# State updates take the bank of the attention values, three matmuls ahead of their merges, and the order of paired heads flips by group

## The chip, the cores and the metric

The kernel runs on one core of one Trainium2 chip. The metric is the device time of one execution in microseconds (us), as the median of several runs. The engines are TensorE (PE: matmuls, with its weight loads as PEld), VectorE (DVE), ScalarE (ACT), GpSimd (POOL) and SyncE (SP, which here issues the weight loads from HBM).

## What is computed

The reference is a two-layer diffusion backbone over 256 latent tokens with 256 context tokens in front, width 1024. Each layer is half an FFN, a token mixer, and another half FFN. The mixer runs four kinds of mixing side by side on slices of one projection: pooling, gated linear attention in two directions, softmax attention, and a Fourier mixing. The change is in the gated linear attention, and its neighbour is the softmax attention.

```python
def gla_scan(q, k, v, g, s0):          # gated linear attention, in chunks of 64
    ...
    def step(S, inp):
        qi, ki, vi, gi = inp
        b = jnp.cumsum(gi.astype(jnp.float32), axis=2)
        b_last = b[:, :, -1:, :]
        S_new = jnp.exp(b_last[:, :, 0, :, None]) * S + jnp.einsum('bhck,bhcv->bhkv', kf * jnp.exp(b_last - b), vf)
        o_inter = jnp.einsum('bhck,bhkv->bhcv', qf * jnp.exp(b), S)
        diff = b[:, :, :, None, :] - b[:, :, None, :, :]
        decay = jnp.exp(jnp.where(mask[:, :, None], diff, -jnp.inf))
        A = jnp.einsum('bhik,bhjk,bhijk->bhij', qf, kf, decay)
        return S_new, o_inter + jnp.einsum('bhij,bhjv->bhiv', A, vf)

def gqa_mix(qc, kc, vc, ql, kl, vl, q_g, k_g, cos, sin, ctx_out):
    ...
        s = jnp.einsum('bqkgd,bskd->bkgqs', q_blk, keys).astype(jnp.float32) * scale
        p = jax.nn.softmax(s, axis=-1).astype(vals.dtype)
        return jnp.einsum('bkgqs,bskd->bqkgd', p, vals)

def token_mix(pc, pl, ...):
    gc, gl = gla_mix(cp[1:7], lp[1:7], gla_wa, gla_ba, gla_norm, ctx_out)
    ac, al = gqa_mix(cp[7], cp[8], cp[9], lp[7], lp[8], lp[9], q_g, k_g, cos, sin, ctx_out)
    y_lat = jnp.concatenate([pool_mix(lp[0], pool_w, pool_scale), gl, al, fnet_mix(lp[10], fnet_w)], axis=-1)

def reference(x, c, ctx, ...):
    for i in range(DEPTH):             # 2 layers; the second leaves the context out behind its mixer
        x = half_ffn(x, ...)
        pl = adaln(x, norm_g[i, 1], ml[3], ml[4]) @ w_in[i]
        yc, yl = token_mix(pc, pl, ...)
        x = x + ml[5] * (yl @ w_out[i])
        x = half_ffn(x, ...)
```

## The kernel before

All activations stay on the chip with features on the 128 partitions. A large float32 product is made as three matmuls of rounded parts (high by high, low by high, high by low). The weights stream from HBM in 1 MB tiles `raw`, which ACT casts to `hi` and DVE subtracts to `lo`. The program is written as Python generators, and a scheduler then reorders instructions on each engine by data dependences and its own estimate of times. After that each engine runs its own list strictly in order and waits for others by semaphores.

PE writes into eight PSUM banks of 128 x 512 floats. In a mixer the banks are handed out by name: `mm` has banks 0 and 1, `pa` 2 and 3, `sc` 4 and 5, `pt` bank 6 and `aux` bank 7. `bank(tag)` takes the next bank of that name in turn, and whoever writes it must wait until all readers of its previous contents are done.

`drive()` interleaves three streams of a mixer.

- `levels()`: for seven block sizes, `scores()` multiplies decayed keys and queries (`E`) for two heads at a time into the two `pa` banks (L813), and DVE merges each bank into the head's matrix `AT` by a predicated copy (L857). Each block size has a group for heads 0 and 1 and a group for heads 2 and 3. A matmul of one head goes to one bank, of the other head to the other bank, alternately.
- `att_units()`: softmax attention. Scores `sc` (L913), softmax on DVE and ACT into `pr` (L895 to L900), transposes into bank `pt` (L921), copied by ACT to `pT` (L923), and the product with the values `pv` into bank `aux` (L930), copied by ACT (L936).
- `dense()`: the projections. `proj_tm` does 24 matmuls `ptm` of 256 columns for a 128-token tile in an `mm` bank (L672 to L674), `proj_fm` does 24 matmuls `pfm`. Behind the pooling's projections come the state updates `states(0)` and `states(1)`, then the output gate `og` (four `ptm` tiles in the first mixer, each read by ACT as a silu, L987) and the Fourier input `u`.

`states(d)` makes three products `pus` of direction d (L748). DVE masks each into `S` (L750) and adds the decayed previous state (L752).

When the streams are done, `outputs()` makes `pog` from the states and `AT` (L873, L875), normalises it by a chain ACT square, DVE sum, POOL power, two DVE products (L882 to L886), and transposes it as `pty` (L1007). `fnet()` makes `pwz`, `pab` and `pyf`. When the last `y` is written, the mixer's pools close, and the output projection `po` over `w_out` begins, whose third `raw` tile takes the memory set free.

In the first mixer four token tiles count (512 columns in a merge), in the second two (256).

Of the kernel before, what the change touches and what calls it, by code (L numbers as in the profile page):

```python
# [13 lines left out]
ALU = mybir.AluOpType  # L14
# [75 lines left out]
def backbone_kernel(ctx: ExitStack, tc: tile.TileContext, a: dict, out: bass.AP):  # L90
    nc = tc.nc
    V, A, TE, SY = nc.vector, nc.scalar, nc.tensor, nc.sync
# [8 lines left out]
    def nm(s):  # L101
        uid[0] += 1
        return f"{s}_{uid[0]}"
# [7 lines left out]
    def bank(tag="mm", lab="b"):  # L111
        own = banks[tag]
        taken[tag] = taken.get(tag, -1) + 1
        return ps.tile([P, 512], F32, tag=f"bank{own[taken[tag] % len(own)]}", name=nm(lab), bufs=1)
# [495 lines left out]
    def mixer(l, st):  # L610
# [17 lines left out]
        cm, o_ = {}, 0  # L628
# [68 lines left out]
        for t2 in range(2):  # L697
            pz = bank("pa", lab="pz")
            for k in range(2):
                t = 2 * t2 + k  # L700
# [29 lines left out]
        ORD = ((2, 3, 0), (3, 2, 1))  # L730
        Sst = [[None] * 3 for _ in range(2)]
        kxs = []
        for d in range(2):
            psf = bank("pa", lab="psf")
            for k, t in enumerate(ORD[d]):
                TE.matmul(psf[:, k * P:(k + 1) * P], cm["strf" if d == 0 else "strb"], gtile(t, d),
                          start=True, stop=True)
# [5 lines left out]
        v_ = gp.tile([P, 4, 256], F32, name=nm("v"))  # L743

        def states(d):
            for k, t in enumerate(ORD[d]):
                pu = bank(lab="pus")
                TE.matmul(pu[:, 0:256], kxs[d][:, k], v_[:, t, :], start=True, stop=True)  # L748
                sn = gp.tile([P, 256], F32, tag=f"S{d}{k}", name=nm("S"))
                V.tensor_tensor(sn, pu[:, 0:256], cm["hm"], ALU.mult)  # L750
                if k:
                    V.scalar_tensor_tensor(sn, Sst[d][k - 1], dec[:, d, t:t + 1], sn, op0=ALU.mult, op1=ALU.add)  # L752
                Sst[d][k] = sn
# [50 lines left out]
        def scores(kt, qt, merge):  # L804

            for h0 in (0, 2):
                pas = [bank("pa", lab="pa") for _ in range(2)]
                first = True
                for t in TL:
                    c = slice(t * P, (t + 1) * P)  # L810
                    for b in (1, 0):
                        hp = slice(32 * (h0 + b), 32 * (h0 + b) + 32)
                        ins = TE.matmul(pas[b][:, c], kt[hp, c], qt[hp, c], start=True, stop=True,  # L813
                                        tile_position=(32 * (h0 + b), 0))
                        if not first:
                            tc.keep_in_program_order(ins)
                        first = False
                for b in range(2):
                    merge(AT[h0 + b][:, 0:NT], pas[b][:, 0:NQ].rearrange("p (t q) -> p t q", q=P))
                yield  # L820

# [25 lines left out]
        def levels():  # L847
            for h in range(4):
                AT[h] = gp.tile([P, 4, P], F32, tag="AT", name=nm("AT"), bufs=4)
            ops = level_operands(0)  # L850
            yield from scores(k_, q_, lambda o, pa: A.mul(o, pa, 2.0))
            for li in range(len(LEVELS)):
                kt, qt = ops
                if li + 1 < len(LEVELS):
                    ops = level_operands(li + 1)
                mk = lm[:, li * P:(li + 1) * P][:, None, :].broadcast_to((P, NT, P))
                yield from scores(kt, qt, lambda o, pa, mk=mk: V.copy_predicated(o, mk, pa))  # L857
# [112 lines left out]
        def dense():  # L970

            yield from proj_tm(wload(wi[:, 1312:1568], KB), kv_cb, range(4))
            yield from proj_tm(wload(wi[:, 1056:1312], KB), lambda t, o: prep(t, o, 0, 4), TL)
            yield from proj_tm(wload(wi[:, 512:768], KB), lambda t, o: A.copy(v_[:, t, :], o[:, 0:256]), range(4))
            V.memset(up.rearrange("p a b c -> p (a b) c")[:, :, 0:8], 0.0)
            V.memset(up.rearrange("p a b c -> p (a b) c")[:, :, 264:272], 0.0)
            raw = wload(wi[:, 0:256], KB)
            for j in range(2):
                proj_fm(raw, j * P, lambda o, j=j: A.copy(up[:, j, 0:len(S), 8:264],
                                                          o[:, 0:NQ].rearrange("p (s c) -> p s c", c=NL)), n=NQ)  # L980
                yield
            for d in range(2):
                states(d)
                yield
            og = gp.tile([P, 4, 256], F32, tag="og", name=nm("og"))
            og_.append(og)
            yield from proj_tm(wload(wi[:, 800:1056], KB), lambda t, o: A.activation(og[:, t, :], o[:, 0:256], AF.Silu), TL)  # L987
            V.tensor_tensor(og[:, 0:NT].rearrange("p t (h d) -> p (t h) d", d=64),
                            og[:, 0:NT].rearrange("p t (h d) -> p (t h) d", d=64),
                            rows[:, 0, None, :].broadcast_to((P, 4 * NT, 64)), ALU.mult)  # L990
            yield from proj_tm(wload(wi[:, 1568:1824], KB), lambda t, o: A.copy(u_[:, t, :], o[:, 0:256]), TL)
# [208 lines left out]
```

## Time and profile before

| what | value |
|---|---|
| median of 3 runs | 1729.26 us (1728.55 to 1732.16) |
| profiled execution's own time | 1730.53 us |
| its span, first to last instruction | 1728.8 us |
| busy: PE, DVE, ACT | 98%, 67%, 36% of the span |
| mean granted TensorE clock | 0.990 of full speed |
| first mixer, about | 440 to 597 us |
| second mixer, about | 1390 to 1500 us |

The profile is of one execution. Its times are used for the sums, and the median of the runs is 1.27 us below that execution's own time. The busy share of PE includes time in which a matmul stands in the pipeline behind a wait, so a stretch with 100% busy can still be slower than another with the same work.

### The profile page before, as it was taken

How to read it: one execution, taken by the hardware profiler on the slowest of the kernel's cores; microseconds unless marked ns; L12 is line 12 of the kernel's file. 1: busy time of each engine (PE TensorE's matmuls, PEld its weight loads, DVE VectorE, ACT ScalarE, POOL GpSimd, SP SyncE). 2: the span in 40 equal slices, each digit the busy share in tenths (PEclk: the TensorE clock that was granted, in tenths of full speed). 3: DMA queues.
4: the chain of work that ended last, by engine and by line, in shares of the span. 5: the costliest groups of instructions: out<-in, count | busy, mean ns of one | idle time of the engine just before them, and what ended most of it. 6: DMA issues, size and time to landing. Idle time of an engine off the chain costs nothing.

```text
span 1728.8 us, 23296 instructions
## 1 busy us (share of the span) xinstructions
PE 1686.6 (98%) x9487; PEld 1444.3 (84%) x9487; DVE 1154.7 (67%) x1715; ACT 617.9 (36%) x947; POOL 31.2 (2%) x40
## 2 busy tenths in 40 slices
PE   6999999999999999999999999999999999999998
PEld 5788888888977888888888898888888897899998
DVE  7788788788776667776776674544554578565554
ACT  6422222223744434212212242222222374554443
POOL 0000000000100000000000000000000010000000
PEclk9999999999998999999999999999999999999999
DMA  9665566444120335554554245454442321365551
GB/s 300 199 197 193 170 195 194 150 133 134 50 73 25 96 100 171 174 167 146 171 164 141 85 134 171 145 167 139 138 162 71 96 89 61 122 194 174 194 159 62
DMA packets 203160, 246.60 MB, mean 143 GB/s; under 512 B 9043, under 2 KB 184542, under 8 KB 203052
## 3 DMA queue, kind: packets, MB, share of 16 engines
q1 hardware_dynamic: 202596, 244.61, 44.7%
q8 instruction: 74, 1.21, 0.3%
q0 software_dynamic: 176, 0.38, 0.1%
q14 instruction: 34, 0.28, 0.0%
q10 hardware_dynamic: 280, 0.12, 0.0%
HBM read 244.04 MB, written 1.05 MB: 142 GB/s over the span
## 4 chain that ended last, share of the span: by engine, by line
PE 91%; DVE 3%; DMA 2%; ACT 1%; issue 1%; SPq 1%; POOL 0%; POOLq 0%; DVEq 0%; ACTq 0%
PE po L298 9%; PE po L300 9%; PE po L299 9%; PE pu L300 8%; PE pu L298 8%; PE pu L299 8%; PE pg L300 7%; PE pg L298 7%; PE pg L299 7%; PE ptm L672 2%; PE ptm L674 2%; PE ptm L673 2%; PE pa L813 2%; DMA big<-in_w_mod_dram 1%; PE pg L482 1%; PE pg L483 1%
## 5 line engine op out<-in xcount | busy, mean ns | idle before, releaser
L264 ACT CAST hi<-raw 128x1024 fp32r<-128x1024 f32 (+1 forms) x291 | 297.0, 1026 | 835.8 <-PE po L299 284.4
L265 DVE TENSOR_TENSOR lo<-raw,hi 128x1024 fp32r<-128x1024 f32 (+1 forms) x291 | 346.0, 1192 | 147.2 <-ACT hi L264 142.7
L337 DVE SCALAR_TENSOR_TENSOR acc<-wmb,scc,acc 128x1024 f32<-128x1024 f32 x196 | 249.8, 1281 | 77.0 <-DMA wmb<-in_w_mod_dram 76.1
L298 PE MATMUL po<-hh,hi 128*128 128x512 f32 (+1 forms) x740 | 263.5, 357 | 0.0
L299 PE MATMUL po<-hl,hi 128*128 128x512 f32 (+1 forms) x740 | 262.9, 356 | 0.0
L300 PE MATMUL po<-hh,lo 128*128 128x512 f32 (+1 forms) x740 | 262.7, 356 | 0.0
L300 PE MATMUL pu<-xh,lo 128*128 128x512 f32 (+1 forms) x664 | 242.3, 365 | 0.0
L298 PE MATMUL pu<-xh,hi 128*128 128x512 f32 (+1 forms) x664 | 242.2, 365 | 0.0
L299 PE MATMUL pu<-xl,hi 128*128 128x512 f32 (+1 forms) x664 | 242.2, 365 | 0.0
L300 PE MATMUL pg<-xh,lo 128*128 128x512 f32 (+1 forms) x632 | 230.6, 365 | 0.0
L299 PE MATMUL pg<-xl,hi 128*128 128x512 f32 (+1 forms) x632 | 230.4, 365 | 0.0
L298 PE MATMUL pg<-xh,hi 128*128 128x512 f32 (+1 forms) x632 | 230.4, 364 | 0.0
L299 PEld LDWEIGHTS po<-hl,hi 128*128 128x128 f32 x740 | 139.7, 189 | 21.1
L300 PEld LDWEIGHTS po<-hh,lo 128*128 128x128 f32 x740 | 139.6, 189 | 21.1
L298 PEld LDWEIGHTS po<-hh,hi 128*128 128x128 f32 x740 | 139.5, 189 | 21.0
L300 PEld LDWEIGHTS pu<-xh,lo 128*128 128x128 f32 x664 | 125.2, 189 | 21.1
L299 PEld LDWEIGHTS pu<-xl,hi 128*128 128x128 f32 x664 | 125.2, 189 | 21.0
L298 PEld LDWEIGHTS pu<-xh,hi 128*128 128x128 f32 x664 | 125.2, 188 | 20.8
L446 DVE SCALAR_TENSOR_TENSOR xT<-po,gate,xT 128x256 f32<-128x256 f32 x168 | 74.7, 479 | 96.1 <-PE po L300 96.0
L299 PEld LDWEIGHTS pg<-xl,hi 128*128 128x128 f32 x632 | 119.2, 189 | 20.0
L300 PEld LDWEIGHTS pg<-xh,lo 128*128 128x128 f32 x632 | 119.2, 189 | 19.8
L298 PEld LDWEIGHTS pg<-xh,hi 128*128 128x128 f32 x632 | 119.2, 189 | 19.8
(255 smaller groups left out, 2309.9 us busy)
## 6 DMA issues: line engine op xcount, KB each, us to landing
wmb<-in_w_mod_dram SPq DMA_DIRECT2D x128, 512.0 KB, 4.2
raw<-in_ffn_wg_dram SPq DMA_DIRECT2D x44, 1024.0 KB, 5.3
raw<-in_ffn_wu_dram SPq DMA_DIRECT2D x44, 1024.0 KB, 7.1
raw<-in_ffn_wd_dram SPq DMA_DIRECT2D x32, 1024.0 KB, 5.2
raw<-in_w_in_dram SPq DMA_DIRECT2D x14, 1024.0 KB, 5.9
raw<-in_ffn_wd_dram SPq DMA_DIRECT2D x16, 768.0 KB, 4.4
big<-in_w_mod_dram SPq DMA_DIRECT2D x16, 512.0 KB, 8.1
raw<-in_w_out_dram SPq DMA_DIRECT2D x8, 1024.0 KB, 7.6
```

The costliest lines, as they stand in the source:

```text
L264: i0 = A.copy(hi[:, 0:n, :], raw[:, 0:n, c0:c0 + P])
L265: i1 = V.tensor_tensor(lo[:, 0:n, :], raw[:, 0:n, c0:c0 + P], hi[:, 0:n, :].bitcast(F32), ALU.subtract)
L298: TE.matmul(o, wh[:, kb, :], mh, start=st, stop=False)
L299: TE.matmul(o, wh[:, kb, :], al[:, k0 + kb, tok0:tok0 + n], start=False, stop=False)
L300: TE.matmul(o, wl[:, kb, :], mh, start=False, stop=sp_)
L337: ins = V.scalar_tensor_tensor(acc[v], wm, scc[:, kb, v:v + 1], acc[v], op0=ALU.mult, op1=ALU.add)
L446: V.scalar_tensor_tensor(xT[:, m, c], o[:, c], gt[:, m, s:s + 1], xT[:, m, c], op0=ALU.mult, op1=ALU.add)
L482: TE.matmul(o[:, c], wh[:, kb, :], ah[:, kb, c], start=(kb == 0), stop=False)
L672: TE.matmul(oo, xh[:, kb, ts], wh[:, k, :], start=(kb == 0), stop=False)
L673: TE.matmul(oo, xh[:, kb, ts], wl[:, k, :], start=False, stop=False)
L674: TE.matmul(oo, xl[:, kb, ts], wh[:, k, :], start=False, stop=(kb == KB - 1))
L813: ins = TE.matmul(pas[b][:, c], kt[hp, c], qt[hp, c], start=True, stop=True, tile_position=(32 * (h0 + b), 0))
```

## The change

In `states(d)` the three products of a direction no longer take the next `mm` bank each. They take two tiles of bank `aux`, which is a single bank: the first two products are the two halves of the first tile, the third is the first half of the second tile. All three matmuls are written ahead of the three merges. In `scores()` the order in which the two banks of a group are filled and merged is no longer always second, first for the matmuls and first, second for the merges. It is now the same for both, and flips between the group of heads 0 and 1 and the group of heads 2 and 3.

```diff
         def states(d):
+            pus = [bank("aux", lab="pus") for _ in range(2)]
+            pus = [pus[0][:, 0:256], pus[0][:, 256:512], pus[1][:, 0:256]]
             for k, t in enumerate(ORD[d]):
-                pu = bank(lab="pus")
-                TE.matmul(pu[:, 0:256], kxs[d][:, k], v_[:, t, :], start=True, stop=True)
+                TE.matmul(pus[k], kxs[d][:, k], v_[:, t, :], start=True, stop=True)
+            for k, t in enumerate(ORD[d]):
                 sn = gp.tile([P, 256], F32, tag=f"S{d}{k}", name=nm("S"))
-                V.tensor_tensor(sn, pu[:, 0:256], cm["hm"], ALU.mult)
+                V.tensor_tensor(sn, pus[k], cm["hm"], ALU.mult)
                 if k:
                     V.scalar_tensor_tensor(sn, Sst[d][k - 1], dec[:, d, t:t + 1], sn, op0=ALU.mult, op1=ALU.add)
                 Sst[d][k] = sn
@@
             for h0 in (0, 2):
                 pas = [bank("pa", lab="pa") for _ in range(2)]
                 first = True
+                turns = (0, 1) if h0 else (1, 0)
                 for t in TL:
                     c = slice(t * P, (t + 1) * P)
-                    for b in (1, 0):
+                    for b in turns:
                         hp = slice(32 * (h0 + b), 32 * (h0 + b) + 32)
                         ins = TE.matmul(pas[b][:, c], kt[hp, c], qt[hp, c], start=True, stop=True,
                                         tile_position=(32 * (h0 + b), 0))
                         if not first:
                             tc.keep_in_program_order(ins)
                         first = False
-                for b in range(2):
+                for b in turns:
                     merge(AT[h0 + b][:, 0:NT], pas[b][:, 0:NQ].rearrange("p (t q) -> p t q", q=P))
```

Since the scheduler decides the lists, the two built kernels were compared list by list. They hold the same instructions but for ACT, which has 21 loads of activation tables instead of 17, the four more in the first mixer. The lists of SP and POOL are equal. PE, DVE and ACT differ in the middle of the first mixer and from the middle of the second mixer to its end.

**PE in the first mixer.** Before, behind the last projection `pfm` of the pooling, PE's list holds scores, level matmuls `pa`, state matmuls `pus` and transposes `pt`, and no projection matmul `ptm` until all of them are issued (row 2375):

```order
2330 L913 MATMUL sc_4199<-qkT_3419 128x512
2331 L813 MATMUL pa_4232<-E_3951 128x128
2333 L921 MATMUL pt_4136<-base,pr_4125 128x128 x4
2340 L748 MATMUL pus_4243<-v_3414,kx_3400 128x256
2341 L748 MATMUL pus_4247<-v_3414,kx_3400 128x256
2342 L921 MATMUL pt_4143<-base,pr_4132 128x128 x4
2343 L813 MATMUL pa_4297<-E_4150 128x128
2353 L748 MATMUL pus_4252<-v_3414,kx_3400 128x256
2355 L813 MATMUL pa_4374<-E_4150 128x128
2363 L921 MATMUL pt_4217<-base,pr_4206 128x128 x4
2367 L813 MATMUL pa_4471<-E_4289 128x128
2375 L672 MATMUL ptm_4319<-hi_4311,xh_3125 128x256
```

After, the `ptm` of the output gate begin five rows behind the scores and stand between all the others:

```order
2330 L916 MATMUL sc_4199<-qkT_3419 128x512
2331 L749 MATMUL pus_4243<-v_3414,kx_3400 128x256
2332 L924 MATMUL pt_4136<-base,pr_4125 128x128 x4
2333 L749 MATMUL pus_4243<-v_3414,kx_3400 128x256
2334 L672 MATMUL ptm_4317<-hi_4309,xh_3125 128x256
2337 L816 MATMUL pa_4231<-E_3951 128x128
2345 L672 MATMUL ptm_4317<-hi_4309,xh_3125 128x256
2348 L924 MATMUL pt_4143<-base,pr_4132 128x128 x4
2364 L749 MATMUL pus_4244<-v_3414,kx_3400 128x256
2381 L816 MATMUL pa_4295<-E_4150 128x128
2399 L924 MATMUL pt_4217<-base,pr_4206 128x128 x4
2420 L816 MATMUL pa_4371<-E_4150 128x128
```

Between rows 2330 and 2420 of the new list stand 65 `ptm`, where the old list has none up to row 2375. The state matmuls of the second direction have moved behind the first `pv`. From the `sc` in row 2567 on, the two lists are equal again to the mixer's end.

**ACT in the same place.** Before, the exponentials of the softmax and of the levels stand together, and the silus of `og` come behind the copy of `pv`:

```order
279 L839 ACTIVATE E_4289<-E_4289 128x1024
280 L923 COPY pT_4222<-pt_4217 128x512
281 L842 ACTIVATE E_4465<-E_4465 128x512
282 L898 ACTIVATE pr_4352,mx_4349<-sc_4345,mx_4349 128x256
285 L936 COPY xqk_3418<-pv_4257 128x256
286 L987 ACT_TABLE_LOAD
287 L987 ACTIVATE og_4308<-ptm_4319 128x256
```

After, three silus stand between exponentials, and each change of function brings a table load:

```order
279 L990 ACT_TABLE_LOAD
280 L990 ACTIVATE og_4306<-ptm_4317 128x256
281 L842 ACT_TABLE_LOAD
282 L842 ACTIVATE E_4287<-E_4287 128x1024
283 L926 COPY pT_4222<-pt_4217 128x512
284 L990 ACT_TABLE_LOAD
285 L990 ACTIVATE og_4306<-ptm_4383 128x256
286 L901 ACT_TABLE_LOAD
287 L901 ACTIVATE pr_4350,mx_4347<-sc_4343,mx_4347 128x256
```

**PE at the end of the second mixer.** Before, the gated outputs come first (`pog`, from row 6958), and the Fourier products `pyf` come last:

```order
6958 L873 MATMUL pog_11781<-S_11403,qe_11734 128x256
6964 L873 MATMUL pog_11738<-S_11398,qe_11734 128x256
6986 L1079 MATMUL pab_11728<-dn_11673,u_10735 128x256 x4
6992 L1007 MATMUL pty_11752<-base,sq_11745 128x128 x2
6993 L1007 MATMUL pty_11795<-base,sq_11788 128x128 x2
6994 L1087 MATMUL pyf_11769<-ab_11727,wz_11678 128x129 x2
6998 L1087 MATMUL pyf_11757<-ab_11727,wz_11678 128x129 x2
```

After, `pyf` is early and `pog` late, with two matmuls `po` between the last `pog` and the first `pty`:

```order
6974 L1090 MATMUL pyf_11753<-ab_11723,wz_11674 128x129 x2
6980 L1090 MATMUL pyf_11765<-ab_11723,wz_11674 128x129 x2
7004 L876 MATMUL pog_11777<-S_11400,qe_11730 128x256
7009 L878 MATMUL pog_11777<-v_10724,AT_10789 128x64
7010 L299 MATMUL po_11872<-y_11684,hi_11873 128x256
7011 L300 MATMUL po_11872<-y_11683,lo_11874 128x256
7012 L1010 MATMUL pty_11748<-base,sq_11741 128x128 x2
7013 L1010 MATMUL pty_11791<-base,sq_11784 128x128 x2
```

Behind the last transposes the new list has 60 `po` before the first one that needs the third `w_out` tile; the old list has 78 `po` behind its first `pyf`.

## Rows read from the trace of the kernel before

**Rows 1.** The page: the span, and busy time of each engine.

```profile
span 1728.8 us, 23296 instructions
PE 1686.6 (98%) x9487; PEld 1444.3 (84%) x9487; DVE 1154.7 (67%) x1715; ACT 617.9 (36%) x947; POOL 31.2 (2%) x40
```

**Rows 2.** The page: the chain that ended last, by engine.

```profile
PE 91%; DVE 3%; DMA 2%; ACT 1%; issue 1%; SPq 1%; POOL 0%; POOLq 0%; DVEq 0%; ACTq 0%
```

**Rows 3.** Windows, first mixer: busy us of PE, PEld, DVE, ACT, POOL; granted clock.

```profile
520.00:530.00 10.00, 6.65 (x46) 4.36 (x46) 9.94 (x26) 3.23 (x7) 0.00 (x0) 0.87 0.01 2
530.00:540.00 10.00, 10.00 (x72) 8.64 (x73) 6.47 (x19) 2.61 (x8) 0.00 (x0) 0.62 0.00 0
...
580.00:600.00 20.00, 19.02 (x105) 15.84 (x104) 12.57 (x33) 7.58 (x22) 2.99 (x3) 1.00 0.20 62
```

**Rows 4.** The same view, one smaller window, PE alone.

```profile
528.00:536.00 8.00, 7.29 (x34) 0.50 0.00 0
```

**Rows 5.** Timeline of PE: start, length, instructions, idle before them and its releaser.

```profile
515.55 1.13 PE L913 MATMUL sc<-qkT 64*128 64x512 f32 x4
...
520.98 1.76 PE L813 MATMUL pa<-E 32*128 32x128 f32 x16 [0.93 <-DVE AT L857]
...
528.71 1.12 PE L921 MATMUL pt<-base,pr 128*128 128x128 f32 x4 [1.95 <-DVE pr L900]
...
539.97 0.28 PE L672 MATMUL ptm<-hi,xh 128*128 128x256 f32 x1
540.09 0.28 PE L673 MATMUL ptm<-lo,xh 128*128 128x256 f32 x1
...
551.16 1.16 PE L813 MATMUL pa<-E 32*128 32x128 f32 x16
```

**Rows 6.** PE's groups from 515.5 to 539.8: count, busy, mean ns, idle before.

```profile
L813 PE MATMUL pa<-E 32*128 32x128 f32 x64 | 6.8, 327 | 1.2 <-DVE AT L857 0.9
L748 PE MATMUL pus<-v,kx 128*128 128x256 f32 x12 | 4.6, 502 | 0.1
```

**Rows 7.** Timeline of DVE: a pair of level merges, and a state merge.

```profile
523.76 0.42 DVE L750 TENSOR_TENSOR S<-pus,mix 128x256 f32<-128x256 f32 x1
...
524.23 1.32 DVE L857 COPY_PREDICATED AT<-lm,pa 128x512 f32<-128x512 uint8 x2
```

**Rows 8.** Timeline of ACT around one table load.

```profile
544.59 0.37 ACT L923 COPY pT<-pt 128x256 f32<-128x256 f32 x1
544.97 1.28 ACT L898 ACT_TABLE_LOAD   x1
546.27 0.47 ACT L898 ACTIVATE pr<-sc,mx 128x256 f32<-128x256 f32 x1
```

**Rows 9.** PE's waits from 1450 to 1510, second mixer: total, times, longest.

```profile
PE po L298 <- ACT hi L264: 2.1, 2, 1.7
PE pv L930 <- ACT pT L923: 0.7, 1, 0.7
PE pab L1079 <- DVE y L1053: 0.6, 1, 0.6
PE pt L921 <- DVE pr L900: 0.5, 1, 0.5
```

**Rows 10.** The end of the second mixer: timelines of PE, DVE, SP, ACT.

```profile
1495.09 0.60 PE L1007 MATMUL pty<-base,sq 128*128 128x128 f32 x4
1499.35 0.42 DVE L1016 TENSOR_TENSOR y<-yy,y 128x256 fp32r<-128x256 f32 x1 [0.53 <-ACT y L1015]
1507.33 2.94 ACT L264 CAST hi<-raw 128x1024 fp32r<-128x1024 f32 x3 [3.07 <-DMA raw<-in_w_out_dram]
1508.42 0.39 PE L298 MATMUL po<-y,hi 128*128 128x256 f32 x1 [1.67 <-ACT hi L264]
```

**Rows 11.** Windows in the second mixer, all engines as in rows 3.

```profile
1450.00:1460.00 10.00, 8.96 (x77) 6.15 (x78) 9.81 (x27) 4.72 (x10) 0.00 (x0) 1.00 0.26 91
...
1512.00:1514.00 2.00, 2.00 (x11) 2.00 (x11) 1.76 (x3) 0.06 (x1) 0.00 (x0) 0.52 0.01 3
```

## The prediction, made blind

> **What bounds the kernel now.** I read the page first. PE is busy 1686.6 of 1728.8 us [rows 1], and the chain that ended last runs over PE for 91% [rows 2]. So only two things can pay here: PE's idle time, and stretches in which PE works slower than it could. Windows of 10 us find the second kind in one place that the change touches, the middle of the first mixer [rows 3]: from 520 to 530 PE is busy 6.65 of 10 us while DVE is busy 9.94, and the granted clock drops to 0.87 and then to 0.62 on average. The finer window shows a plain 0.50, the 1.2 GHz level, from 528 to 536 [rows 4]. What PE did before the clock fell is in the timeline [rows 5]: it idled 0.93 us at 520.05 for a merge of DVE, and 1.95 us at 526.76 for a softmax product of DVE. A group of `pa` that takes 1.16 us in a full stretch (551.16) takes 1.76 us at 520.98, still at full clock, so it holds waits inside itself as well; there are two such groups. No `ptm` starts in the whole stretch until 534.63, though the gate's 96 of them need nothing from the levels. The loss is thus one of order: PE's list holds only work that hangs on DVE there.
>
> The second mixer has no such hole. Its waits ahead of the last transposes add up to 1.8 us, and the longest comes at its end: 2.1 us for the cast of a `w_out` tile [rows 9].
>
> **What the present loss is worth.** The stretch runs from the scores at 515.55 to the first full-speed `ptm` at 539.97 [rows 5], 24.4 us. Its losses, added up:
> - idle, 0.93 + 1.95 = 2.9 us [rows 5];
> - clock, (1 - 0.87) x 10 + (1 - 0.62) x 10 = 5.1 us [rows 3], less about 0.6 for the low clock that falls on the idle time, so 4.5;
> - waits inside the two slow full-clock groups of `pa`, 2 x (1.76 - 1.16) = 1.2 [rows 5].
>
> That makes 8.6 us. The six `pus` stand at a mean of 502 ns a record [rows 6], and how much of that is waiting and how much half clock the row doesn't part. I allow up to 1.5 us, 12 records by about 0.12. The loss is 8.6 to 10.1 us.
>
> **What the new order does with it.** `pus` leaves the `mm` banks, so the gate's `ptm` no longer stand behind DVE's state merges, and 65 of them now lie between the scores and the group of `pa` that came last before DVE's worst backlog (row 2420). One `ptm` starts 0.12 us after another (539.97, 540.09 [rows 5]), so that is 7.8 us of work that needs no DVE result. I walked the list: scores 1.1, two `pa` groups 2.3, the three first `pus` about 1.3, three `pt` about 1.5, the second scores 0.6, `ptm` 7.8. PE reaches row 2420 at about 515.55 + 14.6 = 530.1. DVE ended the last merge it needs at 524.23 + 1.32 = 525.6 before [rows 7]. In the new list DVE has other work ahead of it and my walk puts this end at 530.3, so PE waits 0.2 to 0.3 us there. Later one `pt` waits about 0.65 us for its softmax. The third `pus` must wait for DVE's two reads of the first tile. They stand ahead of the level merges in DVE's new list and end at about 521.2 in the walk, while PE comes at about 522.2: no wait. So 0.9 us of stalls stay, and no idle time of the kind that came before the fall of the clock.
>
> Gain of the first mixer: 8.6 to 10.1, middle 9.4, less 0.9, so **8.5 us**. The end of this mixer has another 0.98 us of PE idle (19.02 of 20 [rows 3]). Its list is the same, so I count nothing for it, and up to +1 for the range. The flip of head order turns two waits of a group into one, for the bank that is merged last. Both merges of a pair take 1.32 us together [rows 7], so the flip is worth at most half of that wherever PE waits at a group, and PE did so once for 0.9 us. It is inside the 9.4.
>
> **The second mixer.** Here the `ptm` also move ahead, but the states come late, and DVE is as full as before (9.81 of 10 [rows 11]). My walk finds these waits of PE: 0.25 for the third `pus` of direction 0 (two S merges), 0.4 for that of direction 1, 0.6 where `pv` needs bank `aux` back from the last S, then 1.0 and 1.6 at the two `pty`, which come behind only two `po` after `pog`. Sum 3.9 us against 1.8 us before. Ahead of the second `pty` the new list has also the two `pyf` (1.6 us) and 18 of the 78 `po` (2.1). Before, `pty` ended at 1495.5. Now 1495.5 + 1.6 + 2.1 + 3.9 - 1.8 = 1501.3, less one `pus` and what the later start of PE takes off its waits for DVE, about 1.5: 1499.8. Its copies then end the mixer near 1500.5, against 1499.77 before [rows 10]. The cast of the third `w_out` tile came 7.6 us behind that end and let PE go on 1.1 us later (1508.42 [rows 10]), 8.7 us in all, and the 60 `po` that PE has left take only 7.2 of them. So PE goes on at about 1509.2, 0.8 us later, and of the second wait for a cast, 0.4 of the 2.1, most goes away. Price **0.5 us**. Bounds: a walk without PE's cost of changing between groups ends the mixer 2.4 us early (gain 2.4); with 0.2 us of hand-off at each of five new waits, and the clock falling for 3.4 us at half as it did around 1512 to 1514 behind the 1.67 us gap [rows 11], it costs 1.0 + 1.7 more (loss 3.2).
>
> **ACT's table loads.** The four more lie in the first mixer. One costs 1.28 us, starting right behind the copy's end at 544.96 and followed by the exponential at 546.27 [rows 8]. Together 5.1 us of an ACT that is busy 3.2 and 2.6 us of 10 in the two windows [rows 3]. Nothing that PE waits for stands behind more than one of them in my walk, so the price is nothing. Without that cover a `pt` waits 1.3 us. The Trainium skill, "ScalarE: Activation LUTs", section What ACT_TABLE_LOAD costs, says more: about 1283 ns for the load and about 1380 ns of drain, 2.66 us for every switch. The row agrees with the load and shows no drain, since the copy, the load and the exponential touch. By the page three switches ahead of one `pt` of the second mixer would come 3 x 1.38 = 4.1 us later, and the sum would be 1725.4 as an estimate, against 1721.3 by the row.
>
> **The sum.** The profiled execution took 1730.53 us, its span 1728.8 and 1.7 around it; the median of the runs is 1.27 less, 1729.26. 1730.53 - 8.5 + 0.5 = 1722.5 for such an execution, and 1729.26 - 8.0 = **1721.3** for the median. By the bounds: -10.1 - 1 - 2.4 gives 1715.8, -7.7 + 3.2 gives 1724.8; both ends at once are unlikely, so the forecast's own range is 1717 to 1724.5.
>
> **The rivals.**
> 1. *Given back later.* The waits in the second mixer are longer than walked, and the clock falls there as it did at 527. For it: five new waits on a DVE that is full. Against: no wait in my list but the last is over 1 us, and each stands between `ptm`. Price: 4 us of waits, or a half-clock stretch of 8 to 10 us at half (4 to 5): 1721.3 + 4 = 1725.3, up to 1728. Chance 0.13.
> 2. *ACT is late.* If a switch of tables holds ACT twice as long as its 1.28 us row, a `pT` copy of the second mixer that stands behind three switches comes 3.8 us later. PE reaches the transpose behind it with the copy just done in the walk, so it would wait about that: 1725.1. Against: the touching rows of ACT [rows 8]. Chance 0.05. The page named above is the one that speaks for it.
> 3. *Nothing comes of it.* DVE's 9.94 of 10 us [rows 3] is unchanged work. If PE merely waits at later groups, the idle moves and the clock falls as before: 1728 to 1730. Against: right behind the hole DVE has only 6.47 of 10 us to do [rows 3], so 7.8 us of other work for PE lets it catch up. Chance 0.08.
> 4. *Slower: the one bank.* Place: the third `pus` of each direction, and behind it PE's whole list, `ptm` too. If DVE reaches the two S merges as late as before (524.2 [rows 7]) PE waits 2.0 us each time, in four directions 8 us, and `pv` stands behind the last. That alone eats the gain (1721.3 + 8 = 1729.3). With one fall of the clock of 5.1 us, as the waits of 0.93 and 1.95 brought before, it is 1734.4. It decides from waits of about 3 us each. Against: DVE's new list has these merges first. Chance 0.06.
>
> **How the numbers follow.** The forecast has 0.68. What a measurement of this kernel can tell from no change is about 0.2%, 3.5 us: faster is below 1725.8, slower above 1732.7. Faster: 0.68, plus 0.07 of rival 1 and 0.03 of rival 2, 0.78. Same: 0.06 of rival 1, 0.02 of rival 2, 0.08 of rival 3, 0.16. Slower: 0.06. The range 1717 to 1728 takes the forecast but for 0.04 at its low end, and rivals 1 and 2: some 0.82.
>
> **What would show it.** In the profile after: a granted clock of 1.00 in all windows from 510 to 550; `ptm` between the `pa` groups; PE's waits there under 1.5 us in sum; what stands behind in the mixer 8 to 9 us earlier; 21 table loads of 1.28 us each, touching their neighbours. In the second mixer: waits at the second `pty` and at the `w_out` cast near 2 us each, and no long half-clock stretch. I am wrong if the clock still falls between 515 and 545, if a third `pus` waits over 2 us, or if PE stands at a `pt` for ACT's copies.

## The result, and the profile after

The changed kernel takes 1719.78 us (1719.44 to 1720.49, 4 runs) against 1728.9 us beside it: ratio 0.9945, 95% interval 0.9928 to 0.9962. That is 9.1 us faster, where 8.0 were forecast. A later set of runs gave 0.9951 (0.9938 to 0.9963).

The page of the changed kernel, span and busy times as in [rows 1]:

```profile
span 1718.7 us, 23296 instructions
PE 1679.9 (98%) x9487; PEld 1441.5 (84%) x9487; DVE 1154.8 (67%) x1715; ACT 623.1 (36%) x951; POOL 31.4 (2%) x40
```

PE is busy 6.7 us less for the same instructions: of the 10.1 us that the span lost, most is not idle time, but a PE that works faster or waits less inside its groups. The windows that answer to [rows 3] say where:

```profile
520.00:530.00 10.00, 10.00 (x89) 9.10 (x88) 9.01 (x22) 8.83 (x13) 0.00 (x0) 1.00 0.01 2
530.00:540.00 10.00, 10.00 (x104) 8.63 (x103) 6.66 (x20) 7.93 (x18) 0.00 (x0) 1.00 0.01 2
...
580.00:600.00 20.00, 19.07 (x91) 15.46 (x90) 8.59 (x18) 6.43 (x14) 0.00 (x0) 1.00 0.51 171
```

The hole is gone. PE is busy 10 of 10 us where it was 6.65, and the granted clock is at its upper level, 2.4 GHz, throughout. PE's timeline over the same work, as in [rows 5], shows no idle time, and between the rows stand `ptm`:

```profile
514.28 1.13 PE L916 MATMUL sc<-qkT 64*128 64x512 f32 x4
...
517.20 1.16 PE L816 MATMUL pa<-E 32*128 32x128 f32 x16
...
520.96 0.59 PE L749 MATMUL pus<-v,kx 128*128 128x256 f32 x2
...
523.38 1.16 PE L816 MATMUL pa<-E 32*128 32x128 f32 x16
...
529.09 0.71 PE L816 MATMUL pa<-E 32*128 32x128 f32 x6
529.72 0.66 PE L924 MATMUL pt<-base,pr 128*128 128x128 f32 x4
```

A full group of `pa` takes 1.16 us, as it did before only where nothing held it. The third `pus`, at 520.96, does not wait.

To measure the first mixer, take the distance from the first `ss` ahead of it to the first `pwz` near its end. In PE's timeline of the kernel before:

```profile
416.64 0.28 PE L405 MATMUL ss<-base,ssacc 128*128 128x1 f32 x2
571.19 1.03 PE L1071 MATMUL pwz<-df 128*128 128x256 f32 x4
```

And of the changed kernel:

```profile
417.03 0.28 PE L405 MATMUL ss<-base,ssacc 128*128 128x1 f32 x2
561.11 1.03 PE L1074 MATMUL pwz<-df 128*128 128x256 f32 x4
```

154.55 us became 144.08, 10.5 less. Of that 0.9 us is lost again at the mixer's end. The two longest of PE's waits from 440 to 640 of the changed kernel (total, times, longest) lie there:

```profile
PE pog L876 <- DVE sq L888: 0.9, 1, 0.9
PE po L298 <- ACT y L1018: 0.7, 1, 0.7
```

In the second mixer new waits have come, PE from 1370 to 1500:

```profile
PE pty L1010 <- DVE sq L889: 3.0, 2, 1.5
...
PE po L298 <- ACT y L1012: 0.5, 1, 0.5
PE pv L933 <- DVE S L752: 0.4, 1, 0.4
...
PE pus L749 <- DVE S L752: 0.4, 1, 0.4
```

Behind the two waits at `pty` the clock is at its lower level, 1.2 GHz, for 6 us (window, PE busy, granted clock):

```profile
1488.00:1490.00 2.00, 0.44 (x2) 0.95 0.00 0
1490.00:1496.00 6.00, 4.95 (x22) 0.50 0.58 184
```

### The profile page after: what moved, and what is told of

Same layout as the page of the kernel before. It is cut to its first block, busy times and chain, and to the rows that moved or that the text cites. A ratio compares the mean times of both kernels' runs of the same rounds, so it can differ in the third digit from the quotient of the medians.

```text
span 1718.7 us, 23296 instructions
## 1 busy us (share of the span) xinstructions
PE 1679.9 (98%) x9487; PEld 1441.5 (84%) x9487; DVE 1154.8 (67%) x1715; ACT 623.1 (36%) x951; POOL 31.4 (2%) x40
## 3 DMA queue, kind: packets, MB, share of 16 engines
HBM read 244.04 MB, written 1.05 MB: 143 GB/s over the span
## 4 chain that ended last, share of the span: by engine, by line
PE 93%; DVE 2%; DMA 2%; ACT 2%; issue 0%; POOL 0%; SPq 0%; POOLq 0%; DVEq 0%; ACTq 0%
PE po L298 9%; PE po L299 9%; PE po L300 9%; PE pu L299 8%; PE pu L300 8%; PE pu L298 8%; PE pg L300 7%; PE pg L299 7%; PE pg L298 7%; PE ptm L672 2%; PE ptm L674 2%; DMA big<-in_w_mod_dram 2%; PE ptm L673 2%; PE pa L816 2%; PE pg L482 1%; PE pg L483 1%
```

## The experiments

Theory A, the prediction's: the gain is filler, gate matmuls that stand between PE's waits for DVE. Its rivals: B, the flip pays by itself; C, three matmuls ahead pay, whatever the bank; D, only leaving the `mm` banks pays. The first four kernels take the change apart.

**The flip alone.**

```diff
+                turns = (0, 1) if h0 else (1, 0)
...
-                    for b in (1, 0):
+                    for b in turns:
...
-                for b in range(2):
+                for b in turns:
```

> The kernel before with the flip of the head order alone; pus stays in the mm banks, each right before its merge. In PE's list of the first mixer no ptm stands before the third group of pa behind the scores (18 ptm come behind it and 26 more before pv). Theory A, that the gain of the change is filler (gate matmuls between the groups that wait for DVE, so no idle time and no fall of the clock): PE still waits near 1 us at the second or third group and the granted clock still falls below 0.8 in one 10 us window between 515 and 545; 1725 to 1729 us, a gain of 0 to 4. Rival B, that the flip pays by making one wait of two in every group of both mixers: a gain of 7 to 9, 1720 to 1722 us.

1725.73 us, ratio 0.9982 (0.9973 to 0.9991). That lies in A's range, though A gives no reason for the 3.1 us that it gains by the ratio. As A said, the hole stays and the clock falls in two windows (from 524 to 534 it is 0.66 on average).

```profile
520.00:530.00 10.00, 6.66 (x48) 4.63 (x49) 9.94 (x26) 3.06 (x7) 0.00 (x0) 0.80 0.01 2
530.00:540.00 10.00, 10.00 (x90) 9.49 (x89) 3.58 (x11) 4.36 (x9) 0.00 (x0) 0.86 0.00 0
```

But a group of `pa` that has waited for DVE now takes 1.16 us, as in a full stretch, where it took 1.76 before [rows 5]:

```profile
520.24 1.16 PE L814 MATMUL pa<-E 32*128 32x128 f32 x16 [1.29 <-DVE AT L858]
```

**The states alone, without the flip.**

```diff
-                turns = (0, 1) if h0 else (1, 0)
...
-                    for b in turns:
+                    for b in (1, 0):
...
-                for b in turns:
+                for b in range(2):
```

> The changed kernel without the flip; pus in bank aux, three ahead of the merges. In PE's list of the first mixer 10 ptm stand behind the first group of pa, and ptm stand between all later groups. Theory A (filler): granted clock 1.00 from 510 to 550 and nearly the whole gain, 1719 to 1722 us. Rival B (the flip): the gain is gone, 1727 to 1729 us.

1726.71 us, ratio 0.9985 (0.9976 to 0.9994): slower by 5 to 8 us than A said, and nearly what B said. Yet the windows agree with A: no idle time, clock 1.00.

```profile
520.00:530.00 10.00, 10.00 (x83) 9.08 (x82) 9.94 (x24) 5.25 (x9) 0.00 (x0) 1.00 0.01 2
530.00:540.00 10.00, 10.00 (x97) 8.29 (x95) 4.56 (x14) 6.64 (x13) 0.00 (x0) 1.00 0.01 2
```

So PE did the same work more slowly while it was fully busy at full clock. The timeline of this kernel shows how, at one group of `pa`:

```profile
523.02 0.28 PE L674 MATMUL ptm<-hi,xl 128*128 128x256 f32 x1
523.23 0.48 PE L815 MATMUL pa<-E 32*128 32x128 f32 x2
523.64 0.39 PE L672 MATMUL ptm<-hi,xh 128*128 128x256 f32 x1
523.87 0.29 PE L673 MATMUL ptm<-lo,xh 128*128 128x256 f32 x1
523.99 0.28 PE L674 MATMUL ptm<-hi,xl 128*128 128x256 f32 x1
...
524.32 1.15 PE L815 MATMUL pa<-E 32*128 32x128 f32 x14
525.40 0.49 PE L915 MATMUL sc<-qkT 64*128 64x256 f32 x2
```

Each matmul has two records here. The group's first matmul stands alone, then come four `ptm`, then the other seven. Fourteen records take 1.08 us (524.32 to 525.40). In the changed kernel all sixteen take 1.09 (523.38, and the next row starts at 524.47): two matmuls of two heads run at the same time on different rows of the array. A matmul that is cut off from its partner takes 0.41 us (523.23 to 523.64) and makes the rest of its group only 0.01 us shorter, and the return to `ptm` costs another 0.1 (0.23 from 523.64 to 523.87, where the next `ptm` starts 0.12 later). The windows view of the line of `pa` alone, from 440 to 575, for this kernel:

```profile
440.00:575.00 135.00, 24.87 (x256) 18.96 (x256) 1.00 0.17 56
```

And the same 256 records in the changed kernel:

```profile
440.00:575.00 135.00, 20.52 (x256) 16.52 (x256) 1.00 0.18 56
```

That is 4.35 us more. PE's list cuts the groups of the first mixer into 31 pieces (a piece is a run of `pa` with no other matmul in it) here, 21 in the changed kernel and 26 in the kernel before, so a cut costs about 0.44 us and the changes of shape around it. This gives a theory K: without the flip a group waits twice, once for each bank, and the scheduler fills the second wait with `ptm` and parts the pair. With the flip the first matmul goes to the bank that is merged last, and the group stays whole.

The two waits can be seen in the kernel before, in the group at 520.98, where nothing fills the second one. Its first matmul goes alone when the first of DVE's two merges is done, and the others start 0.60 us behind it, when the second is (timelines of DVE, and of PE in the windows 520.9 to 521.5 and 521.6 to 522.7):

```profile
520.21 1.32 DVE L857 COPY_PREDICATED AT<-lm,pa 128x512 f32<-128x512 uint8 x2
520.98 0.48 PE L813 MATMUL pa<-E 32*128 32x128 f32 x2 [0.93 <-DVE AT L857]
521.58 1.15 PE L813 MATMUL pa<-E 32*128 32x128 f32 x14
```

In the program the kernel before, too, fills first the bank that it merges last. If DVE merged in that order, the first matmul would wait for the second merge, and the others behind it for nothing more. It goes ahead of that merge, so the scheduler has swapped the two merges in DVE's list.

The Trainium skill, "TensorE: Matmul & The Clock Gate", section The mechanism, says that matmuls on different row groups of the array overlap. This trace agrees: of the changed kernel's sixteen records, two start within the first 0.02 us of the group (timeline of the window 523.38 to 523.40), where of the lone matmul's two only one starts in its first 0.02 us:

```profile
523.38 0.38 PE L816 MATMUL pa<-E 32*128 32x128 f32 x2
```

**The two tiles in the `mm` banks.**

```diff
-            pus = [bank("aux", lab="pus") for _ in range(2)]
+            pus = [bank(lab="pus") for _ in range(2)]
```

> The changed kernel with the two tiles of a direction in the mm banks instead of aux; flip and three matmuls ahead of the merges are kept. In PE's list of the first mixer the first 23 ptm stand only behind all six pus and two groups of pa. Theory A (filler; the bank matters because ptm uses mm too): one wait of about 1 us stays at the second group, a part of the gain is lost, 1721 to 1726 us, with or without a fall of the clock. Rival C, that putting three matmuls ahead of their merges is what pays, whatever the bank: the whole gain, 1719 to 1721 us. Rival D, that only leaving the mm banks pays: no gain, 1727 to 1730 us.

1722.78 us, ratio 0.9966 (0.9954 to 0.9979). Between C and D, in A's range. PE idled 1.8 us at `pa`, 0.9 at `sc` and 0.6 at `pus`, but the clock held:

```profile
520.00:530.00 10.00, 7.21 (x62) 5.74 (x62) 9.94 (x26) 3.27 (x8) 0.00 (x0) 1.00 0.01 2
```

**The flip, and a tile of bank `aux` for each product right before its merge.**

```diff
-                pu = bank(lab="pus")
+                pu = bank("aux", lab="pus")
```

The diff is against the kernel with the flip alone.

> The flip, and each pus in a tile of bank aux of its own right before its merge, so that each matmul of a direction waits for the merge of the one before it. ptm stand between all groups of pa in the first mixer, with 5 ptm ahead of the first group. Theory A (filler): the first mixer gains as in the changed kernel, clock 1.00 from 510 to 550, and the waits at pus are small because the list puts many ptm between them; 1718 to 1723 us. Rival C (three ahead is what pays): a wait of 1 to 2 us at each later pus, 1724 to 1730 us.

1715.49 us, ratio 0.9917 (0.9903 to 0.9930): below A's range of 1718 to 1723, and C fell. It equals the changed kernel in the first mixer: from `ss` at 417.82 to `pwz` at 561.68 are 143.86 us. The rest comes at the end of the second mixer, where its list has 36 `po` between the last `pog` and the first `pty`:

```profile
1481.76 1.00 PE L876 MATMUL pog<-v,AT 128*128 128x64 f32 x8
1486.93 0.60 PE L1008 MATMUL pty<-base,sq 128*128 128x128 f32 x4
```

No wait at `pty`, and the clock is 1.00 from 1480 to 1500. Three matmuls ahead of the merges are not needed for the gain. With the changed kernel's list they go with two `po` there.

**The change in one mixer alone.** The edits give each mixer its own version of both functions (in the other kernel `l == 1`):

```diff
+            new = l == 0
+            if new:
+                pus = [bank("aux", lab="pus") for _ in range(2)]
...
+                if not new:
+                    pus[k] = bank(lab="pus")[:, 0:256]
+                    TE.matmul(pus[k], kxs[d][:, k], v_[:, t, :], start=True, stop=True)
...
+                turns = ((0, 1) if h0 else (1, 0)) if l == 0 else (1, 0)
+                for b in (turns if l == 0 else range(2)):
```

> The change in the first mixer alone; the second mixer has PE's list of the kernel before, row by row. By the prediction's price of 0.5 us for the second mixer this is the faster of the two: 1719 us. By the trace of the changed kernel, in which the stretch from the second mixer's first pz to the sum of squares behind it is 2.2 us shorter than before (124.0 against 126.3): 1721 to 1723 us.

1718.15 us, ratio 0.9939 (0.9927 to 0.9951): the prediction's price holds, and the reading of the trace falls.

> The change in the second mixer alone; the first mixer has PE's list of the kernel before. By the prediction's price: 1729 to 1730 us, no gain, the first mixer's clock falls as before. By the trace of the changed kernel: 1726 to 1728 us, a gain of about 2.

1729.55 us, ratio 1.0009 (1.0000 to 1.0018), 0 to 3 us slower. The hole of the first mixer is there again:

```profile
520.00:530.00 10.00, 7.58 (x60) 5.17 (x60) 9.94 (x22) 3.67 (x7) 0.00 (x0) 1.00 0.01 2
530.00:540.00 10.00, 9.07 (x42) 7.62 (x42) 8.69 (x25) 2.61 (x7) 0.00 (x0) 0.52 0.00 0
```

Why had the trace misled me? The first of these two kernels has the list of the kernel before in its second mixer, row by row, and still took 3.4 us less from the first `pz` to the `ss` behind the mixer (122.9 against 126.3). Half of it is the wait for the cast of a `w_out` tile, which comes from HBM: 2.1 us in the kernel before [rows 9], and with the same list here, PE from 1440 to 1500:

```profile
PE po L298 <- ACT hi L264: 0.4, 1, 0.4
```

The other 1.7 us is the half-clock stretch behind that wait in the kernel before (clock 0.83 on average from 1510 to 1520); the kernel with the change in the first mixer alone has a clock of 1.00 up to the end of the distance, at 1509.68. So the waits for `w_out` and the half-clock stretches differ between executions, and a distance in one execution is uncertain by a few us where it holds one of them. Another half-clock stretch lies in the adaptive norm ahead of the first mixer, in some executions and not in others. PE's windows of the changed kernel:

```profile
420.00:430.00 10.00, 8.46 (x57) 0.83 0.62 185
```

And of the kernel with the change in the first mixer alone, which has the same lists there:

```profile
420.00:430.00 10.00, 8.46 (x69) 1.00 0.62 188
```

The kernel before had 1.00 there too. The distance from `ss` to `pwz` is 142.53 us in the latter's timeline:

```profile
416.75 0.28 PE L405 MATMUL ss<-base,ssacc 128*128 128x1 f32 x2
559.28 1.03 PE L1081 MATMUL pwz<-df 128*128 128x256 f32 x4
```

So without that stretch the first mixer gains 12.0 us to `pwz`.

**The changed kernel in the first mixer, separate tiles in the second.**

```diff
+            pus = [None] * 3
+            if co:                        # the first mixer
...
                 for k, t in enumerate(ORD[d]):
                     TE.matmul(pus[k], kxs[d][:, k], v_[:, t, :], start=True, stop=True)
             for k, t in enumerate(ORD[d]):
+                if not co:
+                    pus[k] = bank("aux", lab="pus")[:, 0:256]
+                    TE.matmul(pus[k], kxs[d][:, k], v_[:, t, :], start=True, stop=True)
```

> The changed kernel in the first mixer; in the second mixer each pus in its own tile of bank aux right before its merge, which puts 36 po between the last pog and the first pty instead of 2. Theory T, that the changed kernel loses time at the two pty, whose chain of ACT, DVE and POOL has nothing to hide it, and in the clock's fall behind it: no wait at pty, no half-clock stretch at 1490, 1714 to 1716 us, as fast as the run with separate tiles in both mixers. Rival U, that the separate tiles gain in the first mixer: no gain here, 1719 to 1721 us.

1715.09 us, ratio 0.9921 (0.9908 to 0.9933), as T said. PE's waits from 1440 to 1500 are 0.5 and 0.2 us:

```profile
PE po L298 <- ACT y L1017: 0.5, 1, 0.5
PE pab L1087 <- DVE y L1061: 0.2, 1, 0.2
```

**Theory K: whole groups without the flip.**

```diff
-                yield from scores(kt, qt, lambda o, pa, mk=mk: V.copy_predicated(o, mk, pa))
+                yield from scores(kt, qt, lambda o, pa, mk=mk: tc.keep_in_program_order(V.copy_predicated(o, mk, pa)))
```

The diff is against the run with the states alone.

> The states of the changed kernel without the flip, but with DVE's merges held in program order, so that each group's first matmul goes to the bank that is merged last. Its list keeps the pa groups nearly whole (22 and 18 pieces of pa in the two mixers; 31 and 27 without the flip, 21 and 17 with it). Theory K, that the flip pays because a group that has one wait instead of two is not cut up by ptm (each cut costs some 0.3 us of PE in changes of shape): the time comes near the changed kernel or below it, 1714 to 1721 us. Rival L, that the alternation of the banks itself pays: as slow as without the flip, 1725 to 1728 us.

1718.97 us, ratio 0.9946 (0.9933 to 0.9960): K holds and L falls. The order of the merges alone is worth 0.39% of 1728, 6.7 us, against the run with the states alone. Its list has 22 pieces in the first mixer, and the 256 records of `pa` take 20.79 us.

**The bank alone, and two tries with merges in program order,** with the changed kernel beside them on one chip.

> The changed kernel itself, as the measure for the other three on the same chip. 0.994 to 0.996 of the kernel before, about 1719 to 1721 us; granted clock 1.00 from 510 to 550, waits of about 1.5 us at each of the two pty of the second mixer.

1720.85 us, ratio 0.9951 (0.9938 to 0.9963). The two waits at `pty` are there again.

The bank alone, against the kernel before:

```diff
-                pu = bank(lab="pus")
+                pu = bank("aux", lab="pus")
```

> The kernel before with one edit: each pus takes a tile of bank aux, right before its merge. No flip, no three ahead. Its list has ptm between the pa groups of the first mixer, but cuts these groups into 32 and 26 pieces (21 and 17 in the changed kernel). Theory K (a cut costs some 0.3 us of PE): clock 1.00 from 510 to 550, no idle time there, and yet 3 to 4 us of the first mixer's gain and 2 to 3 us in the second missing against the run with the flip and separate tiles: 1721 to 1726 us. Rival M, that the bank alone makes the whole gain and the flip only matters where three are ahead: 1714 to 1717 us.

1722.41 us, ratio 0.9963 (0.9950 to 0.9975): inside K's range, and M falls. The clock is 1.00 from 510 to 550 with no idle time, and the first mixer takes 150.3 us (416.73 to 567.01) against 144.0 of the changed kernel beside it (415.44 to 559.40), with 11 pieces more. Its 256 records of `pa` take 25.35 us, 4.83 more, again 0.44 for each cut. The 6.3 us that the first mixer lacks are more than the 3 to 4 that K gave to it.

The bank, and the merges held in order by the edit of the run above:

```diff
+                yield from scores(kt, qt, lambda o, pa, mk=mk: tc.keep_in_program_order(V.copy_predicated(o, mk, pa)))
```

> Separate tiles of bank aux, each pus right before its merge, no flip, but DVE's merges held in program order. 22 and 17 pieces of pa, 12 po between the last pog and the first pty. Theory K: as fast as flip with separate tiles, 1713 to 1717 us. Rival L (the alternation itself pays): 1721 us or more.

1717.66 us, ratio 0.9931 (0.9919 to 0.9943). Not L's 1721, and a little above K's range: PE waits 1.8 us at the two `pty`: 0.25 at the first, behind 12 `po`, and 1.55 at the second, with nothing between the two.

And the same with the flip, whose diff stands at the first run:

> Flip, separate tiles of bank aux, and merges held in program order. 20 and 17 pieces of pa, 12 po ahead of the first pty. Theory K: 1713 to 1717 us, no better than without the flip. It is a try for a version faster than the changed kernel.

1718.16 us, ratio 0.9936 (0.9924 to 0.9948). Missed by 1 us, with the same 1.8 us at `pty` and 0.6 at a `pa`. Of all kernels, the flip with separate tiles has the lowest ratio, 0.9917; the kernel that has them in the second mixer alone, 0.9921, can't be told from it. It is ahead of both given kernels: its interval ends below 0.9938, where that of the changed kernel's second measurement begins, and just overlaps that of the first.

## Why the prediction was right, step by step

- **The hole closes because `ptm` fill it.** Right. Every list with `ptm` between the `pa` groups has a clock of 1.00 from 510 to 550. None has idle time there but the one with the states and merges in program order, 0.9 us at a `pa`, and the one with the `mm` banks. With the flip alone the idle time and the fall of the clock stay.
- **8.5 us in the first mixer.** The direction is right, the size a little low: the kernel with the change there alone gains 1727.82 - 1718.15 = 9.7 us by the medians, 10.5 by the ratio. In the profiles the distance to `pwz` fell by 12.0. My terms were idle 2.9, clock 4.5 and waits inside `pa` groups 1.2. Five cuts fewer (26 to 21) add about 2.2 by 0.44 each, an estimate. That leaves 1.2 of the 12.0, which lies within the 1.5 us that I had allowed for waits at `pus`, whose mean went from 502 ns [rows 6] to 405; no run isolates it. The stalls of 0.9 us from my walk did not come.
- **"It is inside the 9.4", of the flip.** This is the step that failed. I priced the flip by DVE's time for a pair of merges, at most half of 1.32 us per wait. Its worth lies on PE, in pairs that stay together: without it the change gains 2.5 us instead of 9.1. The flip alone gains 3.1 us and the states alone 2.6 by the ratios, together 9.5: each needs the other, since without the flip the `ptm` that fill the waits also cut the groups (31 pieces instead of 26). The 1.2 us that I booked as waits inside two groups are of this kind too. In them DVE's second merge parts the first matmul from its partner. Filler alone turns that into a cut; with the flip the group takes 1.16 us instead of 1.76. I had even counted rows by groups and not seen that the list before cuts them.
- **The end of the first mixer counted at nothing.** Wrong by 0.9 us: 60.45 us from `pwz` to the next `ss` became 61.37.
- **0.5 us lost in the second mixer.** Right in sign, measured at 0 to 3, about 1.5. I had walked waits of 0.25 and 0.4 at the third `pus`, 0.6 at `pv`, 1.0 and 1.6 at the two `pty`. The profile has 0.4 at one `pus`, 0.4 at `pv`, and 1.42 and 1.55 at `pty`. Behind them the clock was low for 6 us, nearly twice the 3.4 that I had put into the upper bound, where my signs had no long half-clock stretch. The wait of near 2 us at the `w_out` cast, on which the price rested, did not come: no wait of `po` for `hi` is in the list. The 0.2 us of hand-off in the upper bound stands in no row; in the kernel before, PE starts 0.05 us after DVE's second merge ends (521.53, 521.58).
- **ACT's four more loads cost nothing.** Right. They touch their neighbours, here around a silu of the gate:

```profile
521.45 0.21 ACT L901 ACTIVATION_READ_ACCUMULATOR pr<-sc,mx 128x1 f32 x1
521.67 1.28 ACT L990 ACT_TABLE_LOAD   x1
522.97 0.39 ACT L990 ACTIVATE og<-ptm 128x256 f32<-128x256 f32 x1
523.37 1.28 ACT L842 ACT_TABLE_LOAD   x1
524.66 1.06 ACT L842 ACTIVATE E<-E 128x1024 f32<-128x1024 f32 x1
```

ACT's busy time rose by 623.1 - 617.9 = 5.2 us, four times 1.28, and no wait of PE for a `pT` copy is in the list. The 2.66 us per switch of the Trainium skill, "ScalarE: Activation LUTs", section What ACT_TABLE_LOAD costs, don't show here; the measurement decides.
- **The rivals.** Rival 1 came in part, as the waits at `pty` and the fall of the clock behind them, within the forecast's own range. Nothing of rivals 2, 3 and 4 is seen: no `pus` waited over 0.4 us.

The sum was -8.5 + 0.5 = -8.0. Measured apart, it is -9.7 to -10.5 and +1.5, so about -8.2 to -9.0; measured together, -9.1. That the sum came so near is partly luck: the flip's worth and the stalls that did not come made the gain larger than forecast, the end of the first mixer and the second mixer made it smaller.

## What to carry to other kernels

Where PE waits for another engine in a stretch, look at what its list holds there before looking at the other engine: here a bank shared between the waiting work and the work that could fill the wait decided it. A busy PE at full clock can still lose time when a scheduler parts small matmuls that run side by side, so count the pieces and compare the busy time of the same records. And compare executions by many runs, not by one distance in a trace, where that distance holds half-clock stretches.

## What was not expected of the hardware

A lone 32-row matmul of two records took 0.41 us; sixteen records in pairs took 1.09 us, and the fourteen that a cut leaves 1.08. And similar waits of PE lower the clock or do not. In the run with the `mm` banks PE waited 0.6, 0.9, 0.3 and 1.6 us between 519 and 530, and the clock stayed at its upper level. Waits of 0.93 and 1.95 us came before its fall in the kernel before and, the same two, in the kernel with the change in the second mixer alone; with the flip alone they were 1.29, 1.05 and 1.22 and two shorter ones. What decides between them stays open.
